# Forgetting attention with the row sums divided out once per pair of heads

## The chip, the cores and the metric

The kernel runs on one NeuronCore of a Trainium2 chip. The metric is device time in microseconds of one launch. A core has TensorE (PE; its weight loads are listed as PEld), VectorE (DVE), ScalarE (ACT), GpSimd (POOL) and SyncE (SP, which here issues the DMAs), each with an instruction queue of its own that is worked off in order.

## The reference

The model is a trunk of two layers on a sequence of 1024 tokens with 1024 channels. Layer 0 is a pooling branch, layer 1 is forgetting attention with 16 heads of 64 channels; both have a gated cross-attention into 256 memory tokens beside them, an output projection and a layer norm. The change lies in the attention of layer 1:

```python
def forgetting_attention(u, k, v, cum):
    # cum: running sum of the log forget gates, (B, S, H)
    def block(args):                      # one block of 128 queries, all keys
        logits = einsum('bqhd,bkhd->bhqk', qi, k) * FOX_HEAD_DIM ** -0.5
        logits = logits + (ci[..., :, None] - cum_k[:, :, None, :])
        logits = where(kpos <= qpos, logits, -inf)
        p = softmax(logits, axis=-1)
        return einsum('bhqk,bkhd->bqhd', p, v)
...
def mixer_sublayer(...):
    y_main = forgetting_attention(u_main, k, v, cum)
    y = concatenate([y_main * silu(g_main), y_mem * silu(g_mem)]) @ w_out
```

The softmax divides each row of probabilities by its sum. Since the sum belongs to a query, it can be divided out of the probabilities or of the attention's output.

## The kernel before

Products that need more precision than bf16 are made of a high part and a low part (two or three matmuls for one). The attention stage lies between about 649 and 1087 us of the profiled span; the output projection, of which parts are drawn into the stage, runs on to the end.

The stage works through 16 heads in 8 pairs, and in each head through 8 query tiles of 128 rows, from tile 7 (1024 keys) down to tile 0 (128 keys). One step of the loop in `fox` is one tile. For a tile, `probs` issues:

- on TensorE, two matmuls for each part of the keys (`mm3`, L231) into one of three PSUM banks "L". A tile with more than 512 keys has two parts, here called first and second; tiles 7 to 4 are of this kind.
- on GpSimd, the mask on the diagonal block of the forget row `R` (L881). The masks are chained: each waits for the custom operation of the tile before.
- on VectorE, a custom operation for each part, which adds the forget row and takes the running minimum (L889; the logits are kept negated, so this is the row maximum). It frees the bank "L". The query-key product number k, in parts, needs the bank that custom operation k − 3 has freed.
- on ScalarE, the exponential (L897) from `p` into one of two PSUM banks "T"; it also gives the row sum.

One step later the functions `inverse` and `behind` follow for that tile: VectorE makes the scaled inverse of the row sum (L907 for two parts, L909 for one, and the reciprocal L910), ScalarE multiplies the probabilities by it and writes them in fp16 as the high half (L918), VectorE writes the rest as the low half (L919), both into a tile "P" (4 buffers), and SyncE issues a DMA transpose of both (L931). Five steps later (LAG = 5), when four tiles of a head are together, `values` multiplies them by the values on TensorE (L948 and L954) into the only PSUM bank "O"; ScalarE (L960) and VectorE (L961) evacuate it into the pair's output tile `o`, channels on the partitions and queries along the row. After a pair's last values `pair_out` multiplies by the gate on GpSimd in four pieces (L970) where the gate is there already (pairs 0, 1, 2, 4 and 7), and stores the result to DRAM (L972). The gates of pairs 3, 5 and 6 come later, in `late_gate` (L985), which reads the stored output back.

Between these, `fill.pump` issues other work to TensorE: slabs of projections (L253) for the coming pairs and gates. TensorE's order is written by hand (`manual_schedule`). The order of the other engines' queues is decided by a planner, from the program's order, costs and due times, and so can differ from the order in the text. The forget rows of a head (`forget_rows`, L866) are a DMA that spreads one row over the 128 partitions; the exchanges of keys within a pair go through the list `due`, which `turn` issues behind the transpose of that step.

After the last pair its output is stored, read back by the output projection (SyncE, L529, tile "T"), split into a high part (ScalarE, L187) and a low part (VectorE, L188) and multiplied on TensorE (L498). Weight pieces for that (`raw`, L453) are fetched and split before, in the same queues.

Of the kernel before, what the change touches and what calls it, by code (L numbers as in the profile page):

```python
# [18 lines left out]
P = 128  # L19
# [80 lines left out]
def trunk_kernel(ctx, tc, x, xT, memT, win, wk, wv0, wv, wmk, wmv, wout, poolw, pscale, lng, lnb, bforget, out):  # L100
# [25 lines left out]
    def sb(shape, tag, bufs, dt=F32, where=None):  # L126
        return (where or pool).tile(shape, dt, tag=tag, name=nm(tag), bufs=bufs)
# [4 lines left out]
    def G(shape=(P, S), dt=F32):  # L132
        return sb(list(shape), "G", 4, dt)
# [30 lines left out]
    def tiny(n, dt=F32):  # L164
        return small.tile([P, n], dt, tag=f"s{n}{dt}", name=nm("s"), bufs=4 if n < 12 else 2)
# [519 lines left out]
    with tc.tile_pool(name="in1", bufs=1) as in1:  # L685
# [180 lines left out]
            nc.sync.dma_start(R, cumd[hd].partition_broadcast(P))  # L866
            return R

        def probs(hd, i, R, sums, inverse, behind):

            q, kx, ky = pairs[hd // 2][hd % 2]
            L = (i + 1) * P
            qs = slice(i * P, L)
            p = MK([P, S], F32)
            with tc.issue_after(masked[-1]) if masked else nullcontext():
                masked.append(  # L880
                    nc.gpsimd.affine_select(R[:, qs], R[:, qs], [[-1, P]], ALU.is_ge, -NEG, base=0, channel_multiplier=1).ins  # L881
                )
            m = tiny(2)
            top = -NEG
            parts = [(0, L)] if L <= NH else [(0, 384), (384, L)] if L == 640 else [(0, NH), (NH, L)]
            for n, (lo, up) in enumerate(parts):
                lg = ps([P, NH], "L", 3)[:, : up - lo]
                mm3(lg, ((q[:, qs], kx[:, lo:up]), (q[:, qs], ky[:, lo:up])))
                nc.vector.tensor_tensor_reduce(p[:, lo:up], lg, R[:, lo:up], 1.0, top, ALU.add, ALU.min, m[:, n : n + 1])  # L889
                top = m[:, n : n + 1]  # L890
                if n == 0:
                    inverse()
            behind()
            es = []
            for n, (lo, up) in enumerate(parts):
                e = ps([P, NH], "T", 2)[:, : up - lo]
                nc.scalar.activation(  # L897
                    e, p[:, lo:up], AF.Exp, bias=top, scale=-1.0, accum_out=sums[:, n, hd % 2, i : i + 1],
                )
                es.append((lo, up, e))  # L900
            return hd, i, es, sums

        def inverse_of(hd, i, n, sums):
            r = tiny(1)
            one, two = (sums[:, n, hd % 2, i : i + 1] for n in range(2))
            if n == 2:
                nc.vector.tensor_scalar(r, one, two, 1.0 / PSCALE, ALU.add, ALU.mult)  # L907
            else:
                nc.vector.tensor_scalar(r, one, 1.0 / PSCALE, None, ALU.mult)  # L909
            nc.vector.reciprocal(r, r)  # L910
            return r

        def halves(hd, i, es, r):

            L = (i + 1) * P
            pair = sb([P, 2 * S], "P", 4, F16)
            for lo, up, e in es:
                nc.scalar.activation(pair[:, lo:up], e, AF.Copy, scale=r)  # L918
                nc.vector.scalar_tensor_tensor(pair[:, L + lo : L + up], e, r, pair[:, lo:up], ALU.mult, ALU.subtract)  # L919
            return hd, i, pair  # L920

        pt, homes = {}, {}

# [39 lines left out]
        bfb = const.tile([P, HEADS], F32, name="bfb")  # L963
        nc.sync.dma_start(bfb, bforget.partition_broadcast(P))

        def pair_out(pr, o, g):

            for k in (3, 2, 1, 0) if g is not None else ():
                cols = slice(k * 2 * P, (k + 1) * 2 * P)
                nc.gpsimd.tensor_tensor(o[:, cols], o[:, cols], g[:, cols], ALU.mult)  # L970
                yield
            nc.sync.dma_start(y1d[pr // 4, :, pr % 4, :], o)  # L972

# [13 lines left out]

        def fox(following, out_proj):
            fill, past, fresh = Fill(), [None] * LAG, [None]
            gs, finished, made, upcoming = {}, iter(()), [], None  # L990

            def gate_ahead(pr):
                gs[pr] = G()
                return gate_units(win[1, 12 + pr], gs[pr], XH, XL)

            ahead_R = forget_rows(0)
            for hd in range(HEADS + 1):
                pr, b = divmod(hd, 2)
                if hd == HEADS:
                    fill.add(lead, SLAB, 0)  # L1000
                if hd < HEADS:
                    if b == 0:
                        o, sums = G(), sb([P, 4 * ST], "sums", 2, F32, small).rearrange("p (n b i) -> p n b i", n=2, b=2)
                        if 0 < pr < 7:
                            fill.add(upcoming, 3 * SLAB, 0)
                        if pr == 0:
                            one, two = (gate_ahead(k) for k in range(2))
                            fill.add(chained((one, 48), (two, 24), (following, 48), (two, 24)), 3 * SLAB)
                        elif pr in (2, 4):
                            fill.add(gate_ahead(pr), SLAB)  # L1010
                        elif pr == 7:
                            gs[7] = G()
                            made.append(gs[7])
                            fill.add(upcoming, SLAB, 0)
                        for late in (3, 5, 6) if pr == 7 else ():
                            fill.add(late_gate(late), SLAB)
                    R, ahead_R = ahead_R, None
                for i in range(ST if hd < HEADS else LAG):
                    tile_of = ST - 1 - i
                    ahead = sum(SHARE[i:]) + (sum(SHARE) if b == 0 else 0)  # L1020
                    part = fill.left * SHARE[i] / (ahead if hd < HEADS else sum(SHARE[i:LAG]))
                    new, split = None, []

                    def inverse():
                        if fresh[0]:
                            old, k, es, of = fresh[0]
                            fresh[0] = old, k, es, inverse_of(old, k, len(es), of)

                    def behind():
                        if fresh[0]:  # L1030
                            split.append(halves(*fresh[0]))
                            fresh[0] = None

                    if b and i == 5 and pr < 7:
                        upcoming = pair_units(pr + 2) if pr < 6 else gate_units(win[1, 19], made, XH, XL)
                    if b and i in (5, 6) and pr < 7:
                        next(upcoming)
                    if i == 2 and hd < HEADS - 1:
                        ahead_R = forget_rows(hd + 1)
                    if pr == 7:  # L1040
                        step = b * ST + i
                        if step in (0, 1, 5, 11):
                            out_proj.fetch_two(land((P, 2, NH)))
                        if step == 9:
                            lead = out_proj.early(land((P, 4, 2 * P)), *in_place(xy, [P, 4, 2 * P]))
                            next(lead)
                    if hd == HEADS and i == 0:
                        out_proj.fetch(12)
                    if hd < HEADS:
                        new = (hd, tile_of, o)  # L1050
                        fresh[0] = probs(hd, tile_of, R, sums, inverse, behind)
                    else:
                        inverse()
                        behind()
                    if pr == 7:
                        out_proj.split((0, 0, 0, 1, 2, 3, 4, 5, 5, 5, 6, 6, 7, 8, 8, 8)[step], True)
                        if step in (12, 13):
                            next(lead)
                    fill.pump(part * FRAC[0])
                    for what in split:  # L1060
                        turn(*what)
                    older = past[0]
                    if older and older[1] % 4 == 0:
                        values(older[0], older[1] // 4, older[2])
                        if older[0] % 2 and older[1] == 0:
                            finished = pair_out(older[0] // 2, older[2], gs.get(older[0] // 2))
                    next(finished, None)
                    fill.pump(part * (1 - FRAC[0]))
                    past = past[1:] + [new]
                run(finished)  # L1070
                if b or hd == HEADS:
                    fill.pump(float("inf"))
                if b and pr < 7:
                    complete(pr + 1)
# [71 lines left out]
```

## Time and profile before

| | |
|---|---|
| median of 3 runs | 1215.22 us (1214.54 to 1215.44) |
| the profiled execution | 1214.61 us |
| its span | 1212.9 us |
| granted TensorE clock | 0.998 |
| matmul instructions on TensorE | 6902 |
| DMA traffic | 178.65 MB |

The span is the time between the first and the last instruction of the profile; the time of the execution lies 1.7 us above it. Rows of the profile name the line of the kernel, the engine, the operation, and the tiles by name (`L` and `T`, `O`, `pj` are PSUM banks, `P` the fp16 probabilities, `G` the outputs and gates, `R` the forget rows).

### The profile page before, as it was taken

The page shows a single profiled execution, that of the slowest core. Times are in us where ns is not written, and L with a number is a line of the kernel's source. Part 1 is how long each engine was busy: PE and PEld are TensorE (multiplying, and loading weights), DVE is VectorE, ACT ScalarE, POOL GpSimd, SP SyncE. Part 2 cuts the span into 40 slices and gives each one's busy share as a digit, 9 for nine tenths or more (in the row PEclk, how much of TensorE's full clock was granted, in tenths as well). Part 3 has the DMA queues.
Part 4 walks back from the last instruction along what each step waited for, and adds up shares of the span by engine and source line. Part 5 has one row for each costly group of instructions (what it writes and reads, how often), then busy time and mean ns, then how long its engine had stood idle before and what let it go on. Part 6 is the DMA issues. An engine that isn't in the chain of part 4 may idle for free. (4 is left out here: it accounts for less than half of the span.)

```text
span 1212.9 us, 19574 instructions
## 1 busy us (share of the span) xinstructions
PE 1185.1 (98%) x6902; PEld 748.8 (62%) x7018; DVE 789.8 (65%) x1861; ACT 607.9 (50%) x1318; POOL 202.6 (17%) x312
## 2 busy tenths in 40 slices
PE   8999999999999999999999999999999999999997
PEld 4567665555555558567775666666666666655553
DVE  6544676375644478357555878777878878775644
ACT  6433654262521125256334777767766777674110
POOL 2000000000000014000004334433334324430000
PEclk9999999999999999999999999999999999999999
DMA  6333554242453335235528788879787989985431
GB/s 237 116 102 88 129 113 156 79 131 70 146 201 104 122 102 181 84 79 107 166 66 171 164 182 177 193 148 195 177 182 181 178 192 212 220 225 197 165 111 46
DMA packets 267410, 178.65 MB, mean 147 GB/s; under 512 B 212272, under 2 KB 225712, under 8 KB 267312
## 3 DMA queue, kind: packets, MB, share of 16 engines
q1 hardware_dynamic: 267312, 177.40, 56.9%
q8 instruction: 55, 0.90, 0.3%
q14 instruction: 43, 0.35, 0.1%
HBM read 94.97 MB, written 22.61 MB: 97 GB/s over the span
## 5 line engine op out<-in xcount | busy, mean ns | idle before, releaser
L253 PE MATMUL pj<-A,w 128*128 128x512 f32 (+1 forms) x1888 | 600.0, 398 | 3.0 <-ACT A L187 0.9
L253 PE MATMUL pj<-A,wl 128*128 128x512 bf16 x951 | 359.7, 379 | 4.6 <-issue 0.5
L253 PEld LDWEIGHTS pj<-A,w 128*128 128x128 f32 x976 | 180.5, 188 | 45.6 <-ACT A L187 2.1
L253 PEld LDWEIGHTS <-w 128*128 128x128 bf16 x992 | 95.8, 98 | 123.9 <-issue 36.4
L253 PEld LDWEIGHTS <-wl 128*128 128x128 bf16 x992 | 97.4, 98 | 94.3 <-issue 6.0
L897 ACT ACTIVATE T<-MK,s 128x512 f32<-128x512 f32 x192 | 111.0, 578 | 58.5 <-DVE s L889 36.5
L919 DVE SCALAR_TENSOR_TENSOR P<-T,s,P 128x512 f16<-128x512 f32 x192 | 111.9, 612 | 31.9 <-ACT P L918 30.4
L918 ACT ACTIVATE P<-T,s 128x512 f16<-128x512 f32 x192 | 102.7, 576 | 49.6 <-issue 27.4
L188 DVE TENSOR_TENSOR wl<-raw,w 128x512 bf16<-128x512 f32 x98 | 72.0, 739 | 82.5 <-ACT w L187 80.3
L498 PEld LDWEIGHTS <-T 128*128 128x128 bf16 x736 | 70.6, 98 | 86.4 <-issue 4.4
L231 PE MATMUL L<-B,B 128*128 128x512 f32 (+3 forms) x384 | 111.0, 390 | 4.7 <-DVE s L889 4.4
L187 ACT CAST w<-raw 128x512 fp32r<-128x512 f32 x106 | 64.7, 618 | 95.3 <-PE pj L253 69.0
L231 PEld LDWEIGHTS L<-B,B 128*128 128x128 f32 x384 | 70.5, 189 | 31.7 <-DVE s L889 12.6
L192 POOL TENSOR_SCALAR A<-A 128x512 bf16<-128x512 f32 (+1 forms) x20 | 16.9, 859 | 433.9 <-ACT A L187 433.9
L889 DVE CUSTOM_DVE_ANT_0 MK<-L,R 128x512 f32<-128x512 f32 (+3 forms) x128 | 72.5, 567 | 6.9 <-DMA R<-cumd 3.4
L881 POOL TENSOR_SCALAR_AFFINE_SELECT R<-R 128x128 f32<-128x128 f32 x128 | 41.5, 330 | 209.5 <-DVE s L889 111.5
L187 ACT CAST T<-T 128x1024 fp32r<-128x1024 f32 x23 | 24.1, 1047 | 97.9 <-DMA T<-y1d 51.9
L198 POOL TENSOR_TENSOR wl<-raw,w 128x512 bf16<-128x512 f32 x54 | 69.2, 1281 | 3.5
L188 DVE TENSOR_TENSOR T<-T,T 128x1024 bf16<-128x1024 f32 x23 | 29.0, 1261 | 42.5 <-ACT T L187 22.5
L197 POOL TENSOR_SCALAR w<-raw 128x512 fp32r<-128x512 f32 x54 | 34.3, 635 | 71.7 <-DMA B<-B 47.3
L498 PE MATMUL L<-B,T 128*128 128x512 bf16 (+1 forms) x165 | 43.3, 391 | 0.2
L889 DVE CUSTOM_DVE_ANT_0 MK<-L,R,s 128x512 f32<-128x512 f32 (+1 forms) x64 | 37.2, 581 | 7.5 <-POOL R L881 4.1
(263 smaller groups left out, 1731.7 us busy)
## 6 DMA issues: line engine op xcount, KB each, us to landing
raw<-in_win_dram SPq DMA_DIRECT2D x96, 256.0 KB, 2.8
raw<-in_wout_dram SPq DMA_DIRECT2D x40, 256.0 KB, 2.7
B<-B SPq DMA_DIRECT2D x32, 256.0 KB, 4.7
R<-cumd SPq DMA_DIRECT2D x16, 512.0 KB, 4.3
y0d<-Y SPq DMA_DIRECT2D x12, 512.0 KB, 3.2
T<-y0d SPq DMA_DIRECT2D x12, 512.0 KB, 3.8
T<-y1d SPq DMA_DIRECT2D x11, 512.0 KB, 4.0
raw<-in_wmk_dram SPq DMA_DIRECT2D x16, 256.0 KB, 2.7
```

The lines of the kernel that those rows point to most:

```text
L187: pin(nc.scalar.copy(hi, src))
L188: pin(by.tensor_tensor(lo[0], src, hi.bitcast(F32), ALU.subtract))
L197: nc.gpsimd.tensor_scalar(hi, src, 1.0, 1.0, ALU.mult, ALU.mult)
L198: nc.gpsimd.tensor_tensor(lo[0], src, hi.bitcast(F32), ALU.subtract)
L231: nc.tensor.matmul(acc, a, b, start=i == 0, stop=i == len(terms) - 1)
L253: nc.tensor.matmul(acc, a, b, start=start, stop=stop)
L498: nc.tensor.matmul(acc, y, w, start=c == 2 and j == firsts[id(acc)], stop=c == 1 and j == lasts[id(acc)])
L881: nc.gpsimd.affine_select(R[:, qs], R[:, qs], [[-1, P]], ALU.is_ge, -NEG, base=0, channel_multiplier=1).ins
L889: nc.vector.tensor_tensor_reduce(p[:, lo:up], lg, R[:, lo:up], 1.0, top, ALU.add, ALU.min, m[:, n : n + 1])
L897: nc.scalar.activation(e, p[:, lo:up], AF.Exp, bias=top, scale=-1.0, accum_out=sums[:, n, hd % 2, i : i + 1],)
L918: nc.scalar.activation(pair[:, lo:up], e, AF.Copy, scale=r)
L919: nc.vector.scalar_tensor_tensor(pair[:, L + lo : L + up], e, r, pair[:, lo:up], ALU.mult, ALU.subtract)
```

## The change

The exponentials are split into high and low fp16 halves with a constant scale (PSCALE), without their row sums. The ScalarE copy therefore moves into `probs`, directly behind the exponential, and the per-tile inverse on VectorE goes. The row sums of both heads of a pair are collected in one tile; `inverse_rows`, in the third step of the next pair, adds the parts, takes 16 reciprocals per partition, transposes them on TensorE into the bank "O", copies them to 16 rows with ScalarE and writes them to DRAM. `inverse_wide`, one step later, reads them back with two DMAs, one for each head, each spread over 64 partitions, into a tile "P"; for pairs 0 to 6 the two loads go through `due`. `pair_out` then has a leading step that does nothing and multiplies each of the four pieces by these inverses on GpSimd, for all eight pairs, ahead of the gate.

```diff
@@ -866,7 +866,7 @@
             nc.sync.dma_start(R, cumd[hd].partition_broadcast(P))
             return R
 
-        def probs(hd, i, R, sums, inverse, behind):
+        def probs(hd, i, R, sums, behind):
 
 
 
@@ -888,8 +888,6 @@
                 mm3(lg, ((q[:, qs], kx[:, lo:up]), (q[:, qs], ky[:, lo:up])))
                 nc.vector.tensor_tensor_reduce(p[:, lo:up], lg, R[:, lo:up], 1.0, top, ALU.add, ALU.min, m[:, n : n + 1])
                 top = m[:, n : n + 1]
-                if n == 0:
-                    inverse()
             behind()
             es = []
             for n, (lo, up) in enumerate(parts):
@@ -898,26 +896,38 @@
                     e, p[:, lo:up], AF.Exp, bias=top, scale=-1.0, accum_out=sums[:, n, hd % 2, i : i + 1],
                 )
                 es.append((lo, up, e))
-            return hd, i, es, sums
-
-        def inverse_of(hd, i, n, sums):
-            r = tiny(1)
-            one, two = (sums[:, n, hd % 2, i : i + 1] for n in range(2))
-            if n == 2:
-                nc.vector.tensor_scalar(r, one, two, 1.0 / PSCALE, ALU.add, ALU.mult)
-            else:
-                nc.vector.tensor_scalar(r, one, 1.0 / PSCALE, None, ALU.mult)
-            nc.vector.reciprocal(r, r)
-            return r
-
-        def halves(hd, i, es, r):
-
             L = (i + 1) * P
             pair = sb([P, 2 * S], "P", 4, F16)
             for lo, up, e in es:
-                nc.scalar.activation(pair[:, lo:up], e, AF.Copy, scale=r)
-                nc.vector.scalar_tensor_tensor(pair[:, L + lo : L + up], e, r, pair[:, lo:up], ALU.mult, ALU.subtract)
+                nc.scalar.activation(pair[:, lo:up], e, AF.Copy, scale=PSCALE)
+            return hd, i, es, pair
+
+        def halves(hd, i, es, pair):
+
+            L = (i + 1) * P
+            for lo, up, e in es:
+                nc.vector.scalar_tensor_tensor(pair[:, L + lo : L + up], e, PSCALE, pair[:, lo:up], ALU.mult, ALU.subtract)
             return hd, i, pair
+
+        inverses = dram.tile([KT, 2 * ST, P], F32, name="inverses")
+
+        def inverse_rows(pr, sums, rows):
+
+            r = sums[:, 0]
+            nc.vector.tensor_tensor(r, sums[:, 0], sums[:, 1], ALU.add)
+            nc.vector.reciprocal(r, r)
+            t = ps([P, NH], "O", 1)[: 2 * ST, :P]
+            nc.tensor.transpose(t, r.rearrange("p b i -> p (b i)"), ident)
+            nc.scalar.copy(rows, t)
+            nc.sync.dma_start(inverses[pr], rows)
+
+        def inverse_wide(pr):
+
+            wide = sb([P, S], "P", 4)
+            for b in range(2):
+                load = wide[64 * b : 64 * b + 64], inverses[pr, ST * b : ST * b + ST].rearrange("i q -> (i q)").partition_broadcast(64)
+                due.append(load) if pr < 7 else nc.sync.dma_start(*load)
+            return wide
 
         pt, homes = {}, {}
 
@@ -963,11 +973,14 @@
         bfb = const.tile([P, HEADS], F32, name="bfb")
         nc.sync.dma_start(bfb, bforget.partition_broadcast(P))
 
-        def pair_out(pr, o, g):
-
-            for k in (3, 2, 1, 0) if g is not None else ():
+        def pair_out(pr, o, g, inv):
+
+            yield
+            for k in (3, 2, 1, 0):
                 cols = slice(k * 2 * P, (k + 1) * 2 * P)
-                nc.gpsimd.tensor_tensor(o[:, cols], o[:, cols], g[:, cols], ALU.mult)
+                nc.gpsimd.tensor_tensor(o[:, cols], o[:, cols], inv[:, cols], ALU.mult)
+                if g is not None:
+                    nc.gpsimd.tensor_tensor(o[:, cols], o[:, cols], g[:, cols], ALU.mult)
                 yield
             nc.sync.dma_start(y1d[pr // 4, :, pr % 4, :], o)
 
@@ -987,7 +1000,7 @@
 
         def fox(following, out_proj):
             fill, past, fresh = Fill(), [None] * LAG, [None]
-            gs, finished, made, upcoming = {}, iter(()), [], None
+            gs, finished, made, upcoming, sums = {}, iter(()), [], None, None
 
             def gate_ahead(pr):
                 gs[pr] = G()
@@ -1000,7 +1013,9 @@
                     fill.add(lead, SLAB, 0)
                 if hd < HEADS:
                     if b == 0:
-                        o, sums = G(), sb([P, 4 * ST], "sums", 2, F32, small).rearrange("p (n b i) -> p n b i", n=2, b=2)
+                        o, past_sums = G(), sums
+                        sums = sb([P, 4 * ST], "sums", 2, F32, small).rearrange("p (n b i) -> p n b i", n=2, b=2)
+                        nc.gpsimd.memset(sums[:, 1], 0.0)
                         if 0 < pr < 7:
                             fill.add(upcoming, 3 * SLAB, 0)
                         if pr == 0:
@@ -1021,11 +1036,6 @@
                     part = fill.left * SHARE[i] / (ahead if hd < HEADS else sum(SHARE[i:LAG]))
                     new, split = None, []
 
-                    def inverse():
-                        if fresh[0]:
-                            old, k, es, of = fresh[0]
-                            fresh[0] = old, k, es, inverse_of(old, k, len(es), of)
-
                     def behind():
                         if fresh[0]:
                             split.append(halves(*fresh[0]))
@@ -1048,22 +1058,28 @@
                         out_proj.fetch(12)
                     if hd < HEADS:
                         new = (hd, tile_of, o)
-                        fresh[0] = probs(hd, tile_of, R, sums, inverse, behind)
+                        fresh[0] = probs(hd, tile_of, R, sums, behind)
                     else:
-                        inverse()
                         behind()
                     if pr == 7:
                         out_proj.split((0, 0, 0, 1, 2, 3, 4, 5, 5, 5, 6, 6, 7, 8, 8, 8)[step], True)
                         if step in (12, 13):
                             next(lead)
                     fill.pump(part * FRAC[0])
+                    if hd and b == 0 and i == 2:
+                        if hd == HEADS:
+                            inverse_rows(pr - 1, sums, G()[: 2 * ST, :P])
+                        else:
+                            inverse_rows(pr - 1, past_sums, o[: 2 * ST, :P])
+                    if hd and b == 0 and i == 3:
+                        inv = inverse_wide(pr - 1)
                     for what in split:
                         turn(*what)
                     older = past[0]
                     if older and older[1] % 4 == 0:
                         values(older[0], older[1] // 4, older[2])
                         if older[0] % 2 and older[1] == 0:
-                            finished = pair_out(older[0] // 2, older[2], gs.get(older[0] // 2))
+                            finished = pair_out(older[0] // 2, older[2], gs.get(older[0] // 2), inv)
                     next(finished, None)
                     fill.pump(part * (1 - FRAC[0]))
                     past = past[1:] + [new]
```

## The prediction

> **What bounds the kernel now.** I read the page first: busy time by engine and the chain of work that ended last.
>
> ```profile
> PE 1185.1 (98%) x6902; PEld 748.8 (62%) x7018; DVE 789.8 (65%) x1861; ACT 607.9 (50%) x1318; POOL 202.6 (17%) x312
> PE 15%; DMA 2%; DVE 1%; issue 1%; POOL 1%; ACT 0%; DVEq 0%; POOLq 0%; SPq 0%; ACTq 0%
> ```
>
> TensorE is busy 98% of the span and the chain is nearly all its own. So no work removed from VectorE shortens anything by itself; it can only shorten a TensorE wait. The next view is therefore TensorE's waits from the start of forgetting attention (640 us) to the end.
>
> ```profile
> PE L L231 <- DVE s L889: 4.4, 13, 0.6
> PE pj L498 <- DVE G L284: 1.5, 1, 1.5
> PE O L948 <- DMA T<-P: 1.4, 1, 1.4
> PE L L498 <- ACT B L187: 0.8, 1, 0.8
> ```
>
> Columns are total us, times, longest. Together these are 8.1 us: thirteen query-key products (L231) wait for a bank that the custom add-and-min (L889) must free, one values product waits for a DMA transpose, two projections wait for their operands. That is the ceiling of what the change can win, about 8 us of 1215, and only if every wait goes. Everything it adds to TensorE, or to a chain that ends in these waits, comes on top.
>
> **Part 1: the inverse of each tile goes (L907, L909, L910).** The groups of instructions between 640 and 1100 us:
>
> ```profile
> L910 DVE RECIPROCAL s<-s 128x1 f32<-128x1 f32 x128 | 20.4, 160 | 2.4
> L907 DVE TENSOR_SCALAR s<-sums 128x1 f32<-128x1 f32 x64 | 13.5, 211 | 26.0 <-ACT T L897 25.9
> L909 DVE TENSOR_SCALAR s<-sums 128x1 f32<-128x1 f32 x64 | 9.4, 147 | 8.0 <-ACT T L897 6.1
> L970 POOL TENSOR_TENSOR G<-G,G 128x256 f32<-128x256 f32 x20 | 15.7, 807 | 28.6 <-DVE G L961 28.6
> ```
>
> Columns behind the bar are busy us, mean ns of one, then the engine's idle us before it and who ended it. Removed are 20.4 + 13.5 + 9.4 = 43.3 us of VectorE work and 25.9 + 6.1 = 32.0 us in which it stood waiting for an exponential. ScalarE's copy (L918 before, L902 after) no longer waits for VectorE, so it follows its exponential at once. On TensorE this touches the 4.4 us at L231 and the 1.4 us at L948. I do not count 4.4 + 1.4 in full: in the new order of VectorE's queue the two subtractions (L909 after) of tile 7, and the evacuation L971, stand ahead of the custom operation of tile 6 at most heads, and they wait for ScalarE's exponential and copy. That was the same wait under another name. I take −1.5 us at heads 4, 8 and 12, where both customs of tile 7 stand early, −1 us at the other heads and −1.4 us for the transpose: −3.9 us. Bounds: −8.1 (every wait goes) to 0.
>
> **Part 2: one transpose per pair on TensorE (L920).** Eight instructions appear. The nearest rows are the mask transposes of 128x128 f32 earlier in the kernel:
>
> ```profile
> L730 PEld LDWEIGHTS T<-ident,T x16: 138/140/142, 618.9 to 624.5; 128*128 128x128 f32 x16
> L730 PE MATMUL T<-ident,T x16: 270/272/273, 619.0 to 624.7; 128*128 128x128 f32 x16
> ```
>
> A transpose lasts 272 ns, weight load 140 ns, and part of both overlaps neighbours. Here only 16 columns are the stationary side, so I take 0.15 us each, 8 x 0.15 = +1.2 us; bounds 0 and 8 x (0.272 + 0.140) = 3.3. The reciprocals for it (L917, L918) stand early in VectorE's queue, so pairs 0 to 6 wait for nothing but the O bank.
>
> **Part 3: the wide inverse and 32 more multiplications on GpSimd (L981), with the masks behind them.** GpSimd works in order. In the new order of its queue, at heads 2, 6 and 10, stand: four multiplications that wait for the wide loads, the mask of tile 0 (L881), four more, then the mask of the next head's tile 7. The loads are two half-size copies of the row broadcast; the rows for them and for the write of the rows:
>
> ```profile
> R<-cumd SPq DMA_DIRECT2D x16, 512.0 KB, 4.3
> cumd<-G SPq DMA_DIRECT2D x7, 8.0 KB, 1.5
> ```
>
> The same place before, at head 2, from the timeline of each engine (start, length):
>
> ```profile
> 712.97 1.83 SPq L931 DMA_TRANSPOSE T<-P  x1
> 715.41 1.42 POOL L970 TENSOR_TENSOR G<-G,G 128x256 f32<-128x256 f32 x2 [0.58 <-DVE G L961]
> 718.53 0.54 POOL L881 TENSOR_SCALAR_AFFINE_SELECT R<-R 128x128 f32<-128x128 f32 x2 [1.70 <-DVE s L910]
> 718.86 0.29 DVE L889 CUSTOM_DVE_ANT_0 MK<-L,R 128x128 f32<-128x128 f32 x1
> 722.23 0.75 DVE L889 CUSTOM_DVE_ANT_0 MK<-L,R,s 128x512 f32<-128x512 f32 x1
> 726.73 0.67 DVE L889 CUSTOM_DVE_ANT_0 MK<-L,R 128x512 f32<-128x512 f32 x1
> 727.47 0.50 PE L231 MATMUL L<-B,B 128*128 128x256 f32 x2 [0.38 <-DVE s L889]
> ```
>
> The wide loads are put behind the transpose of tile 5 on SyncE's queue. Before, it ends issuing at 714.8. An inverse (0.21 + 0.16 us) and the wait before it were ahead of that:
>
> ```profile
> DVE s L907 <- ACT T L897: 25.9, 32, 1.6
> ```
>
> 25.9 / 32 = 0.8 us, so I put the loads 1.2 us earlier, at 713.6, and they land 4.3 us later, at 717.9. Four multiplications at 1.42 / 2 = 0.71 us end at 720.7; with a mask of 0.27 us tile 0's custom starts at 721.0 where it started at 718.86. Four more multiplications end at 723.8 and the mask of tile 7 at 724.1; the second part of tile 7 then starts at 724.1 instead of 722.23, 1.9 us late, and I add 0.3 us for tile 7's subtractions, which now stand ahead of tile 6's custom (part 1). That custom (726.73 before) follows on the same engine, and the query-key product at 727.47 already waits 0.38 us for the bank that it frees. So nothing absorbs the delay: 2.2 us per such head, x 3 heads = +6.6 us. Heads 4, 8, 12 and 14 have one multiplication or none ahead of a mask at the critical place; I count them at 0. Bounds: 0 (the loads land early enough, GpSimd's idle 1.70 us takes the rest) to 3 x 3.5 + 4 x 1.5 = 16.5. I take 6.6 because its rows are of the place itself. The wide loads add half the volume of the sixteen row broadcasts to SyncE's queue; I count no later transposes for that here (the third rival does).
>
> **Part 4: the last pair, where nothing covers.** After the last head there is one path: evacuation, GpSimd, store, load, cast, projection.
>
> ```profile
> 1082.25 0.76 DVE L961 SCALAR_TENSOR_TENSOR G<-O,unscale,G 64x512 f32<-64x512 f32 x1
> 1085.66 0.72 PE L948 MATMUL O<-T,V 128*128 128x128 f16 x10
> 1087.23 3.77 SPq L453 DMA_DIRECT2D raw<-in_wout_dram  x4
> 1087.26 1.14 ACT L194 CAST MK<-MK 128x512 bf16<-128x512 f32 x2
> 1095.36 0.76 DVE L961 SCALAR_TENSOR_TENSOR G<-O,unscale,G 64x512 f32<-64x512 f32 x1
> 1096.19 2.92 POOL L970 TENSOR_TENSOR G<-G,G 128x256 f32<-128x256 f32 x2 [11.70 <-DVE G L961]
> 1096.75 1.76 DVE L188 TENSOR_TENSOR T<-T,T 128x1024 bf16<-128x1024 f32 x1
> 1099.14 0.33 SPq L972 DMA_DIRECT2D y1d<-G  x1
> 1106.77 1.05 ACT L187 CAST T<-T 128x1024 fp32r<-128x1024 f32 x1 [6.34 <-DMA T<-y1d]
> 1108.53 0.81 PE L498 MATMUL L<-R,T 128*128 128x512 f32 x2
> ```
>
> From the store at 1099.14 to the end of the cast at 1107.82 are 8.7 us, and the first projection that reads it starts at 1108.53: 0.7 us of slack. Two delays meet here. On TensorE the transpose of pair 7 uses the O bank, which L961 frees at 1083.0, about 1.6 us after its turn; then its copy to rows (L921) stands behind the casts that end at 1087.26 + 1.14 = 1088.4, and the values product that stood at 1085.66 needs the bank back: in all about +3 us on TensorE. On GpSimd's side the rows are written by SyncE behind the four loads that end at 1091.0, so the wide loads go out at about 1091.5 and land at 1095.8. Then eight multiplications follow where two followed: 8 x 0.72 = 5.8 us, to 1101.6, or up to 1104 if those beside VectorE's work take 2.92 / 2 = 1.46 us as the last two did. Store at 1102 to 1104 instead of 1099.14, that is +2.9 to +4.9, less 0.7 of slack: +2.2 to +4.2. I take +3.3, TensorE's own +3 being beside it and not on top. Bounds +1.5 to +5. The rule for why some of them last twice as long is in the Trainium skill (SBUF — State Buffer, "Who interferes with whom"): a VectorE instruction with two SBUF inputs holds a port that GpSimd needs to read, and the later of the two waits entirely. The trace agrees: the two multiplications of 2.92 us lie beside L188, whose two inputs are both in SBUF. By that rule, with all eight against such work, the store would come at 1095.8 + 8 x 1.46 = 1107.5 and this part would cost 7.7 us, the sum 11.6 us and the time 1226.8, inside the forecast's own range.
>
> **The sum.** −3.9 + 1.2 + 6.6 + 3.3 = +7.2 us. On the profiled execution (1214.61 us, span 1212.9) that is 1221.8; the median of the runs is 0.6 higher, 1215.22, so 1222.
>
> The same sum with the page DMA: Bandwidth & Descriptors ("Two cost components") puts a fixed 2 us on each transfer; that makes the write 0.5 us slower than its row (1.5) and is within the bounds of part 4.
>
> **The rivals.** *Relief on VectorE wins.* The 75 us taken from VectorE's queue (43.3 busy, 32.0 waiting) clear L231's waits and the transpose's, part 3 costs nothing because the loads land before GpSimd comes to them, and the tail costs its lower bound. For it: GpSimd is busy 17% and idles 1.70 us before the very mask. Against: the subtractions ahead of tile 6's custom. It gives −8.1 + 0.5 + 0 + 1.5 = −6 at best, −4.5 with the two projection waits half gone: 1210.5. Chance 0.12.
> *A draw.* The gain is 3.9 and part 3 costs nothing: −3.9 + 1.2 + 3.3 = +0.6, 1215.8. Chance 0.13.
> *GpSimd waits for the loads at every pair.* DMA engines are busy 84.7% of this stage:
>
> ```profile
> q1 hardware_dynamic: 183814, 85.89, 84.7%
> ```
>
> If the wide loads land 2 us later than a row broadcast's median, all seven pairs hold the masks, three by 2.2 + 2 = 4.2 us and four by 1 us: 16.6 + 3.3 + 1.2 − 3.9 = +17.2, 1232.4. It decides from the point where a landing exceeds about 6 us. Chance 0.2.
> The forecast has the rest, 0.55.
>
> **How the numbers follow.** Measurement tells 0.2% (2.4 us) from no change. Slower, above 1217.7: the forecast and the third rival, 0.55 + 0.2 = 0.75; same 0.13, the draw; faster, below 1212.8, 0.12. The range takes in the draw and most of the unknown costs: from 1213.5 (most of the first rival lies below it) to 1231 (the worst part of the last rival above): about 2 in 10 outside. The forecast's own range is 1217.7 to 1227.
>
> **What would show it.** Part 1 right: no VectorE wait for the exponential before a reciprocal, ScalarE's copy no longer released by "issue" or VectorE. Part 2: eight L920 rows with TensorE idle under 0.3 us, but for the last. Part 3: rows of POOL at L981 released by the DMA of the wide tile, masks L881 behind them, customs L889 that wait for POOL, and TensorE waits at L231 growing from 4.4 to about 10 us at heads 3, 7 and 11. Part 4: POOL's last rows end at 1102 to 1104 plus what the stage before has lost, and the projection that reads the last pair starts 3 us later against the last head's end. Wrong: L231's waits shrinking below 4.4 us, or the wide loads landing well before GpSimd turns to them.

## The result and the profile after

The changed kernel takes 1221.76 us (median of 4 runs, 1221.04 to 1222.62) against 1215.27 us (1214.54 to 1215.44) for the kernel before: a ratio of 1.0055, 95% interval 1.0037 to 1.0072. It is slower by more than the 0.2% that can be told from no change, and the time was forecast to 0.3 us. As the experiments show, two terms of the sum were much too small and their errors cancelled, so that this closeness is luck.

The page of the changed kernel, busy time and the chain that ended last:

```profile
span 1220.2 us, 19470 instructions
PE 1188.5 (97%) x6910; PEld 752.9 (62%) x7026; DVE 749.2 (61%) x1621; ACT 595.0 (49%) x1326; POOL 228.6 (19%) x352
PE 77%; DVE 6%; ACT 5%; issue 5%; DMA 4%; POOL 2%; SPq 0%; DVEq 0%; POOLq 0%; ACTq 0%
```

VectorE has lost 40.6 us of work (43.3 were counted), and the chain now leaves TensorE for 23% of the span: it runs through VectorE, ScalarE and the wide loads. TensorE's waits from 640 us to the end (total us, times, longest us):

```profile
PE L L231 <- DVE s L889: 8.8, 8, 2.1
PE O L920 <- DVE G L971: 3.1, 1, 3.1
PE L L498 <- ACT T L187: 1.4, 1, 1.4
```

Before there were 13 short waits at L231, none over 0.6 us; now there are 8, the longest 2.1 us. The other two rows stand at the end of the kernel: the transpose of the last pair waits for the bank O, and the first projection that reads the last pair waits for its cast. The waits of the other engines between 640 and 1106 us show what is behind the first row:

```profile
POOL G L981 <- DMA P<-inverses: 29.7, 7, 16.2
DVE MK L889 <- POOL R L881: 10.0, 10, 2.7
ACT P L902 <- POOL G L981: 6.8, 5, 4.7
```

The second row read before, between 640 and 1100 us:

```profile
DVE MK L889 <- POOL R L881: 6.0, 9, 3.0
```

GpSimd waits for the wide loads (16.2 of the 29.7 us in the last pair), VectorE's custom operations wait for the masks behind them (6.0 us before, 10.0 now), and ScalarE's copies wait for the buffer P that GpSimd still reads.

### The profile page after: what moved, and what is told of

It reads as the page before. It is cut to its first block, busy times and chain, and to the rows that moved or that the text cites. A ratio compares the mean times of both kernels' runs of the same rounds, so it can differ in the third digit from the quotient of the medians.

```text
span 1220.2 us, 19470 instructions
## 1 busy us (share of the span) xinstructions
PE 1188.5 (97%) x6910; PEld 752.9 (62%) x7026; DVE 749.2 (61%) x1621; ACT 595.0 (49%) x1326; POOL 228.6 (19%) x352
## 4 chain that ended last, share of the span: by engine, by line
PE 77%; DVE 6%; ACT 5%; issue 5%; DMA 4%; POOL 2%; SPq 0%; DVEq 0%; POOLq 0%; ACTq 0%
PE pj L253 42%; PE L L231 8%; PE L L498 8%; PE pj L498 6%; PE O L498 2%; DVE MK L889 2%; ACT T L895 2%; PE T L498 2%; DMA P<-inverses 2%; PE L L750 2%; PE pj L231 2%; ACT P L902 2%; DVE P L909 2%; PE T L231 1%; PE O L958 1%
## 5 line engine op out<-in xcount | busy, mean ns | idle before, releaser
L253 PE MATMUL pj<-A,w 128*128 128x512 f32 (+1 forms) x1894 | 606.3, 401 | 2.6 <-ACT A L187 0.5
L909 DVE SCALAR_TENSOR_TENSOR P<-T,P 128x512 f16<-128x512 f32 x192 | 104.6, 554 | 84.6 <-ACT P L902 83.3
L231 PE MATMUL L<-B,B 128*128 128x512 f32 (+3 forms) x384 | 108.5, 387 | 8.8 <-DVE s L889 8.8
L902 ACT ACTIVATE P<-T 128x512 f16<-128x512 f32 x192 | 87.2, 482 | 10.8 <-POOL G L981 6.8
L231 PEld LDWEIGHTS L<-B,B 128*128 128x128 f32 x384 | 71.3, 189 | 32.5 <-DVE s L889 12.3
```

The costliest lines, as they stand in the source:

```text
L231: nc.tensor.matmul(acc, a, b, start=i == 0, stop=i == len(terms) - 1)
L253: nc.tensor.matmul(acc, a, b, start=start, stop=stop)
L902: nc.scalar.activation(pair[:, lo:up], e, AF.Copy, scale=PSCALE)
```

## The experiments

Ratios are to runs of the kernel before on the same chip. The diffs are shortened to the lines that matter. The lag of one kernel behind another is the difference in the start of the same TensorE weight load in both; no weight load is missing from these traces, while some matmuls are.

**Part 1 by itself.** No transposes of the sums, no wide loads and no multiplications by them; the probabilities keep the constant scale, and the division by the row sums is left out:

```diff
-                    if hd and b == 0 and i == 2: ... inverse_rows(...)
-                    if hd and b == 0 and i == 3: inv = inverse_wide(pr - 1)
-                nc.gpsimd.tensor_tensor(o[:, cols], o[:, cols], inv[:, cols], ALU.mult)
```

> The changed kernel without the division by the row sums: no transposes of the sums, no rows in DRAM, no wide loads and no multiplications by them; the rest of part 1 stays (constant scale, no inverse per tile). Theory (the prediction's sum): what is left is the gain of part 1 alone, 3.9 us, and the last pair is as before: 1211.3 us, with TensorE's waits at L231 at 3 us or less. From the lags of the changed kernel the gains at single places add up to about 7 us, so it may be as low as 1208.5. Rival (the relief of VectorE is worth nothing, since TensorE bounds the stage and the subtractions wait where the inverses waited): 1215 us. Rival (constant scale makes the order of VectorE's queue worse, and the loss of the changed kernel is this): 1218 us or more.

Measured: 1200.06 us, ratio 0.9871 (0.9857 to 0.9885). That is a gain of 15.6 us, four times the 3.9 us of the prediction and twice the ceiling that I read from TensorE's waits. All expectations missed it. Its group of query-key products, in the view by line from 640 to 1100 us, has no idle time at all; the row of its weight loads names no releaser any more:

```profile
L231 PE MATMUL L<-B,B 128*128 128x512 f32 (+3 forms) x384 | 106.2, 384 | 0.0
L231 PEld LDWEIGHTS L<-B,B 128*128 128x128 f32 x384 | 72.0, 189 | 20.6
```

In the trace of before the same view has a row that I had not used; the waits of the weight loads are beside it:

```profile
L231 PEld LDWEIGHTS L<-B,B 128*128 128x128 f32 x384 | 70.5, 189 | 31.7 <-DVE s L889 12.6
PEld L L231 <- DVE s L889: 12.6, 21, 1.1
```

The matmuls' row said 4.4 us in 13 waits, the weight loads' row 12.6 us in 21. Going from before to part1_alone, TensorE gains 15.0 us of span, of which some 10 fall to L231: the weight loads' row came much nearer to the prize than the matmuls' row. One wait seen closely: at head 3 the matmul waited 0.38 us by its row (shown in the prediction), and TensorE is 0.65 us further ahead in part1_alone behind it. The rest of the 15.0 us is 1.5 us at the values product that waited for a transpose, and 3 us at the end.

**The inverse on VectorE again, read by nobody.** On top of part1_alone:

```diff
+                if n == 0 and last: inverse_of(*last.pop())   # L907/L909 and L910 as before; r is not used
```

> As part1_alone (1200.1 us; no division at all), but VectorE computes the inverse of each tile again where it stood before, and nobody reads it: 43 us of VectorE work and its waits for the exponential return, while ScalarE's copy keeps its constant scale and its place. It tells apart what part 1 is worth to VectorE's queue and to ScalarE's. Theory (the gain is VectorE's: its queue, in order, frees the banks too late): most of the 15 us comes back, 1209 to 1214 us, L231's waits 3 us or more. Rival (the gain is that ScalarE's copy no longer waits for the inverse, and so the exponential and all behind it come earlier): 1200 to 1203 us.

Measured: 1207.34 us, ratio 0.9941 (0.9927 to 0.9956). It lies between both expectations: about half of part 1's gain (7.3 us) is VectorE's queue. The other half (7.9 us to the kernel before) is put down to ScalarE's copy, which no longer waits for the inverse and stands directly behind the exponential; this is what remains, no run has that half alone. The waits at L231 give the two rows a second comparison:

```profile
PE L L231 <- DVE s L889: 1.4, 4, 0.4
PEld L L231 <- DVE s L889: 5.9, 11, 0.8
```

From here to part1_alone, where both are gone, TensorE gains about 5 us between 640 us and the last head: again the weight loads' row is the nearer one.

**The inverse on GpSimd, in the kernel before.**

```diff
-                nc.vector.tensor_scalar(r, one, two, 1.0 / PSCALE, ALU.add, ALU.mult)
+                nc.gpsimd.tensor_scalar(r, one, two, 1.0 / PSCALE, ALU.add, ALU.mult)
-            nc.vector.reciprocal(r, r)
+            nc.gpsimd.tensor_tensor(r, r, minus, ALU.pow)     # minus: -1.0
```

The inverse of tiles with one part (L909) moves likewise.

> The kernel before, with the inverse of each tile computed on GpSimd (an add or multiply, then a power of minus one) instead of VectorE; the probabilities are scaled as before and there is no wide inverse. Theory (VectorE's queue sets the waits at L231): the relief is there without the division's cost; GpSimd's two small operations of about 0.3 us per tile stand between masks and beside weight splits of 1.28 us, so ScalarE's copy waits longer, but TensorE's waits fall: 1202 to 1209 us. Rival (ScalarE's copy bounds, and GpSimd makes the inverse later still): 1216 to 1225 us, with waits for T<-P on TensorE.

Measured: 1280.23 us, ratio 1.054 (1.0524 to 1.0557): far beyond the rival. The power of one column takes 563 ns on GpSimd where VectorE's reciprocal took 160, and ScalarE's copies wait 115 us for it (two rows, by line and by wait):

```profile
L910 POOL TENSOR_TENSOR s<-s,minus 128x1 f32<-128x1 f32 x128 | 72.1, 563 | 10.0
ACT P L918 <- POOL s L910: 115.0, 123, 2.6
```

VectorE is relieved of the same instructions as in part1_alone, yet TensorE's waits at L231 grow from 4.4 to 50.9 us: the copy's later start outweighs the relief. What the relief alone is worth this run does not show.

**Multiplications whose operand is ready.** The changed kernel, but GpSimd multiplies by the gate or the output itself, so that the division by the row sums is left out:

```diff
-                nc.gpsimd.tensor_tensor(o[:, cols], o[:, cols], inv[:, cols], ALU.mult)
+                nc.gpsimd.tensor_tensor(o[:, cols], o[:, cols], (o if g is None else g)[:, cols], ALU.mult)
```

> The changed kernel, but the 32 new multiplications on GpSimd read a tile that is ready (the gate a second time, or the output itself) instead of the wide inverse; sums, transposes, rows and wide loads stay, nobody reads the wide tile, so the row sums are not divided out. Theory (it is the wait for the loads with masks behind it that costs, not the multiplications): the stage keeps only the transposes (8 x 0.22 us by the spacing of TensorE's weight loads) and some waits for a buffer P, and the end keeps its wait for the bank O: 1204 to 1210 us, L231's waits 2 us or less. Rival (the multiplications themselves delay the masks): 1216 us or more.

Measured: 1208.35 us, ratio 0.9952 (0.9937 to 0.9967), as expected. The 32 multiplications are all there and cost little in the stage: up to the last pair this kernel is 3.9 us behind part1_alone, the changed kernel 16.7 us. So the 12.8 us between are the wait for the wide loads with what stands behind it. TensorE's wait at L231 is 0.6 us. The profiled execution was the slowest of the five (1210.53 us); it loses another 7.0 us to part1_alone in the last pair, in part at a granted clock of 0.57 from 1065 to 1067 us, so its end is not used here.

**The loads one tile earlier, and one tile later.**

```diff
-                    if hd and b == 0 and i == 3:
+                    if hd and b == 0 and i == 2:      # wide_one_step_earlier
+                    if hd and b == 0 and i == 4:      # wide_one_step_later
```

The edit moves the loads of all eight pairs, the last one included.

> The changed kernel with the wide loads issued one tile earlier (behind the transpose of tile 6 instead of tile 5). Theory (GpSimd holds the masks while it waits for the wide tile): the loads land some 3 us earlier, the mask of the next head's tile 7 is out some 2.7 us earlier at heads 7 and 11, and of the 3.2 us lost at each of these some 2 us come back, with 1 us more at heads 5 and 13: 1216 to 1218.5 us, L231's waits 4 to 6 us. Rival (the loss is TensorE's transposes and DMA traffic, not the wait): 1221.8 as the changed kernel. Rival (SyncE now stops at the loads, because the rows are not yet written, and its transposes come late): 1223 us or more, with waits for T<-P on TensorE.

> The changed kernel with the wide loads issued one tile later (behind the transpose of tile 4). In the new order of GpSimd's queue the mask of tile 0 and that of the next head's tile 7 then stand ahead of all eight multiplications. Theory (what costs time is not that the loads are late but which masks stand behind the multiplications): the delays at heads 3, 7 and 11 go, though the loads land later: fox stage some 5 us shorter than in the changed kernel, last pair unchanged, 1216 to 1218 us, L231's waits about 3 us. Rival (the landing of the loads is the cost): each of seven pairs loses up to 3 us more, 1225 to 1235 us.

Measured: earlier 1216.95 us, ratio 1.0016 (1.0005 to 1.0027); later 1215.11 us, ratio 0.9989 (0.9979 to 0.9999). Both are faster than the changed kernel, and the later one more so. That rules out the late landing as a cost by itself: it costs what stands behind it in GpSimd's queue, so an earlier landing helps, and another order of the queue helps more. GpSimd at the end of head 6, in the changed kernel:

```profile
827.27 1.43 POOL L981 TENSOR_TENSOR G<-G,P 128x256 f32<-128x256 f32 x2 [1.90 <-DMA P<-inverses]
828.66 1.43 POOL L983 TENSOR_TENSOR G<-G,G 128x256 f32<-128x256 f32 x2
830.04 0.30 POOL L881 TENSOR_SCALAR_AFFINE_SELECT R<-R 128x128 f32<-128x128 f32 x1
830.30 1.41 POOL L981 TENSOR_TENSOR G<-G,P 128x256 f32<-128x256 f32 x2
831.67 1.43 POOL L983 TENSOR_TENSOR G<-G,G 128x256 f32<-128x256 f32 x2
833.04 0.30 POOL L881 TENSOR_SCALAR_AFFINE_SELECT R<-R 128x128 f32<-128x128 f32 x1
```

and with the loads one tile later:

```profile
823.50 0.54 POOL L881 TENSOR_SCALAR_AFFINE_SELECT R<-R 128x128 f32<-128x128 f32 x2 [1.95 <-DVE s L889]
825.75 1.41 POOL L981 TENSOR_TENSOR G<-G,P 128x256 f32<-128x256 f32 x2 [1.71 <-DMA P<-inverses]
827.12 1.41 POOL L983 TENSOR_TENSOR G<-G,G 128x256 f32<-128x256 f32 x2
```

In the first the masks of tile 0 and of the next head's tile 7 stand behind four and eight multiplications; in the second both are out before the multiplications begin. What follows in the changed kernel, on VectorE and TensorE:

```profile
830.37 0.29 DVE L889 CUSTOM_DVE_ANT_0 MK<-L,R 128x128 f32<-128x128 f32 x1 [1.25 <-POOL R L881]
833.38 0.75 DVE L889 CUSTOM_DVE_ANT_0 MK<-L,R,s 128x512 f32<-128x512 f32 x1 [0.42 <-POOL R L881]
836.20 1.29 DVE L909 SCALAR_TENSOR_TENSOR P<-T,P 128x512 f16<-128x512 f32 x2 [2.07 <-ACT P L902]
838.07 0.67 DVE L889 CUSTOM_DVE_ANT_0 MK<-L,R 128x512 f32<-128x512 f32 x1
838.80 0.50 PE L231 MATMUL L<-B,B 128*128 128x256 f32 x2 [2.08 <-DVE s L889]
```

Custom of tile 0, custom of tile 7, its subtractions, custom of tile 6, bank, query-key product: the chain of the prediction, link by link. With the later loads the last row reads 0.53 us instead of 2.08. Up to the last pair that kernel is 9.1 us ahead of the changed kernel (some 5 expected), but its end, expected unchanged, gives 3.3 us back in the profiled execution: TensorE waits there for casts, 1.83 us at 1068.48 and 2.31 us at 1109.01, each time with a granted clock of 0.55 to 0.62 in the 3 us that follow. In the changed kernel, too, behind the long wait comes a second cost, seen in TensorE's windows (length, busy and matmuls, granted clock, DMA share, GB/s):

```profile
836.00:840.00 4.00, 1.92 (x10) 0.97 0.66 187
840.00:843.20 3.20, 3.20 (x9) 0.50 0.83 243
843.20:846.00 2.80, 2.80 (x15) 1.00 1.05 288
```

For 3.2 us the clock is at half, and TensorE falls behind by about another 1.5 us. Head 11 shows the same (clock 0.53 from 949.5 to 952.6).

**The last pair as before.**

```diff
+                if hd < HEADS - 2:                    # heads 14 and 15: inverse per tile, no wide inverse
                     nc.scalar.activation(pair[:, lo:up], e, AF.Copy, scale=PSCALE)
```

> The changed kernel, but heads 14 and 15 are computed as before (inverse of each tile, scaled probabilities, no wide inverse). Theory: the stage up to head 13 keeps its loss, the tail's is gone: the wait of 3.1 us before TensorE's last transpose and the 1.4 us wait for the last pair's cast vanish, 1221.8 - 3.3 = 1218.5 us. Rival (the tail's delay is covered by the projection work that TensorE has there anyway): 1221.5 us.

Measured: 1220.55 us, ratio 1.0039 (1.0025 to 1.0052). The 3.1 us wait at the transpose is gone, but the old inverse costs heads 14 and 15 something again (at head 15 a wait of 1.02 us at L231 instead of 0.41), so only 1 to 2 us come back instead of 3.3.

**A bank of its own for the last transpose.** On top of the later loads:

```diff
-            t = ps([P, NH], "O", 1)[: 2 * ST, :P]
+            t = (ps([P, NH], "O", 1) if pr < 7 else ps([P, NH], "T", 2))[: 2 * ST, :P]
```

with the rows of the last pair one step earlier and its loads one step after them.

> As wide_one_step_later (1215.1 us), but for the last pair the sums are transposed into a bank T, which is free there, one step earlier, and the wide loads are issued one step after that. Theory (the end loses because the transpose and the next values product wait for the only bank O, and because the wide loads stand behind the weight loads): against part1_alone the end lost 8.8 us in wide_one_step_later, and some 5 of them come back: 1209 to 1211 us, no wait at L920 and L958 behind the last head. Rival (the eight multiplications and the store are the end's path whatever TensorE does): 1214 us.

Measured: 1216.05 us, ratio 1.0007 (0.9998 to 1.0016): nothing gained against the later loads, so the theory missed. The time is nearer to the rival, but the rival's path is not what held it. TensorE's waits for the bank are gone, and with the multiplications done the store goes out at 1095.9, 3.3 us earlier than with the later loads; the same work ends in a longer wait for the last cast:

```profile
PE L L498 <- ACT T L187: 3.6, 1, 3.6
```

The cast starts only at 1106.80, 10.9 us after the store (7.6 us before: 1099.14 to 1106.77), because the load that it waits for, issued at 1099.22, lands 7.5 us later (4.0 us in the kernel before). Behind the wait TensorE's clock is at 0.50 from 1108 to 1112 us, and its lag behind part1_alone grows there by 2.3 us more. Why the load took so long was not tried.

**Two of the repairs together.** Later loads for pairs 0 to 6, last pair as before.

> wide_one_step_later and last_pair_as_before together: wide loads behind the transpose of tile 4 for pairs 0 to 6, inverse of each tile for heads 14 and 15. Theory (the places add up): against part1_alone (1200.1 us) the stage up to head 13 costs 6.3 us as in wide_one_step_later, heads 14 and 15 and the end some 4 to 5 us, which is what they cost the kernel before (3.4) and last_pair_as_before (6): 1210 to 1213 us, faster than both kernels. Rival (the end is bound by something else that both versions share): 1215 us.

Measured: 1210.08 us (1209.04 to 1213.38), ratio 0.9964 (0.995 to 0.9978): faster than both kernels, and within what the places added up to.

## Why the prediction was right, and where it was not

| step | predicted | measured |
|---|---|---|
| part 1, inverse of each tile goes | −3.9 (−8.1 to 0) | −15.6 (part1_alone), 12 of it up to the last pair |
| part 2, transposes | +1.2 (0 to 3.3) | +1.8, 1.6 of it up to the last pair |
| part 3, GpSimd behind the wide loads | +6.6 (0 to 16.5) | +12.8, clock included |
| the rest of operands_ready's lag | not counted | +2.3 |
| up to the last pair, net | +3.9 | +4.6 |
| part 4, the last pair, against before | +3.3 (+1.5 to +5) | +2.7 |

The two net rows are TensorE's lag of the changed kernel behind before: 4.6 us at the last head (its product at 1065.32 starts at 1069.94) and 7.3 us at the end of the span.

*Part 1 failed in size.* The step was the ceiling of 8.1 us, summed from the matmuls' waits. A product that waits for its bank holds up its weight load too, and there the row says 12.6 us where the matmuls' row says 4.4; what came back at L231 was some 10. The discount below the ceiling failed as well: the subtractions of tile 7 do stand ahead of tile 6's custom and wait 2.07 us for ScalarE in part1_alone too, yet there TensorE does not wait. An order that looks tight need not be binding.

*Part 3 failed in size, not in kind.* Heads 2, 6 and 10 were named with their queue, and the loads even came earlier than assumed: the first multiplication at head 2 started at 716.18 (717.9 predicted), tile 0's custom at 719.29 (721.0), tile 7's second part at 722.28 (724.1). Head 3 therefore lost only 1.5 us against part1_alone, but heads 7 and 11 lost 3.9 and 3.8, of which about 1.5 each is the half clock. TensorE's waits at L231 came to 8.8 us in all (about 10 predicted), 5.1 of it at these three heads. And head 13, counted at 0, lost 3.0 us. No mask stood behind the multiplications there; it was the buffer that the wide inverse takes from the probabilities, which the prediction did not price. At head 12, on ScalarE and VectorE:

```profile
992.51 0.38 ACT L902 ACTIVATE P<-T 128x256 f16<-128x256 f32 x1 [4.74 <-POOL G L981]
992.93 0.42 DVE L909 SCALAR_TENSOR_TENSOR P<-T,P 128x256 f16<-128x256 f32 x1 [4.70 <-ACT P L902]
993.27 0.28 DVE L889 CUSTOM_DVE_ANT_0 MK<-L,R 128x128 f32<-128x128 f32 x1
```

ScalarE's copy needs one of the four buffers P and waits until GpSimd has read the wide inverse in another; VectorE's subtraction waits for the copy, and the custom of tile 0 for its turn behind that. This is read from the trace; no run gave the wide inverse a buffer of its own. With the later loads head 13 loses as much (3.1 us): there the copies of head 12's last tiles wait for transposes to free a buffer, 1.74 and 1.69 us. Heads 5, 6 and 15 lose 0.8 to 1.4 us each.

*Part 2* was 0.23 us for each transpose by TensorE's spacing (0.15 taken). *Part 4* was right in size and in its places: a wait before the last transpose (3.06 us, predicted some 1.6 and more behind it), the values product after it, the store at 1106.74, which is 1102.1 without the 4.6 us lost before (1102 to 1104 predicted). The write of the last rows landed in 2.3 us and the two wide loads in 5.0 and 5.9 us (1.5 and 4.3 taken; the medians of all pairs are 1.6 and 4.3). The eight multiplications took 7.0 us:

```profile
1099.73 2.35 POOL L981 TENSOR_TENSOR G<-G,P 128x256 f32<-128x256 f32 x2 [16.17 <-DMA P<-inverses]
1103.88 1.43 POOL L981 TENSOR_TENSOR G<-G,P 128x256 f32<-128x256 f32 x2
```

Two take 2.35 us while VectorE subtracts from two operands in SBUF (until 1102.6), and 1.43 us after that. This agrees with the rule of the Trainium skill that the prediction weighed (SBUF — State Buffer, "Who interferes with whom"), but only part of the eight lay beside such work.

So the net up to the last pair came out right by luck, because gain and cost were both taken too small by about as much: 3.9 for 12 us, and 7.8 for 16.7 us. Of the rivals, the relief of VectorE was the true story of part 1, priced at half and coupled with a part 3 that costs nothing; the rival in which GpSimd waits at every pair was the nearest description of part 3.

## What to carry to other kernels

Size a wait of TensorE by the row of its weight loads as well as by that of its matmuls, and where the two differ, test the gain alone before trading it against a cost. When work with a late operand goes into an in-order queue, look for the urgent instruction that is put behind it: starting the operand's transfer later, so that the planner puts the urgent work first, gave back some 7 us here (6.7 by the medians, 8.0 by the ratios). And a staging tile taken from a busy pool of buffers is a wait of its own, to be priced like any other.

## What was not expected of the hardware

After idle gaps of 2.1 and 1.9 us (heads 7 and 11) TensorE ran at about half the clock for some 3.2 us, while after gaps of 1.1 us (head 3), 1.8 us (head 13) and 3.1 us (the last transpose) of the same execution the clock stayed at 1.00. The length of a gap alone does not decide: in the run with the loads one tile earlier, two gaps of 1.86 us at L231 were followed by a clock of 1.00 (836.0 to 839.2) and 0.59 (946.4 to 949.6). The Trainium skill (TensorE: Matmul & The Clock Gate, "What's actually happening") tells of a free-running window of about 3.4 us and puts the slow state behind at least one idle window. The length of the half clock agrees with that, but here gaps of about 2 us were enough, and the measurement decides. What picks the gaps was not tried. The windows behind the gaps at heads 11 and 13 and at the last transpose (columns as above):

```profile
949.50:952.60 3.10, 3.10 (x9) 0.53 1.14 254
1000.90:1004.20 3.30, 3.30 (x16) 1.00 1.19 286
1087.30:1090.60 3.30, 3.30 (x16) 1.00 0.91 280
```
